# A two-layer hybrid encoder on one core: the first gate and up products are opened by token halves with spare buffers, and GpSimd makes the squares of the program's input and their sum

## The chip, the cores and the metric

The kernel runs on one NeuronCore of a Trainium2 chip. The metric is the time of one execution on the device in microseconds (us); a smaller one is better. The kernel before takes 2196.76 us, the median of three runs (2196.46 to 2197.05). Engines are called as in the profile: PE (matmuls), PEld (its weight loads), DVE (VectorE), ACT (ScalarE), POOL (GpSimd) and SP (SyncE, which here only issues DMAs).

## The reference

The input is 512 tokens of 1024 channels; 16 learned meta tokens are added, so that 528 token columns are worked on. Two layers each run a gated feed-forward block, a mixer (gated linear attention beside softmax attention, merged by gates) and a second feed-forward block. The change touches the start of the first feed-forward block alone:

```python
def rmsnorm(x, g):
    y = xf * lax.rsqrt(jnp.mean(xf * xf, axis=-1, keepdims=True) + EPS)
    return (y * g.astype(jnp.float32)).astype(x.dtype)

def swiglu(x, w_gate, w_up, w_down):
    return (jax.nn.silu(x @ w_gate) * (x @ w_up)) @ w_down

for l in range(DEPTH):
    h = h + 0.5 * swiglu(rmsnorm(h, norm_gains[l, 0]), ...)
    ...
```

## The kernel before

Channels lie on the 128 partitions, tokens in the free dimension: `h(c)` is chunk c of eight, 128 x 528 in float32. All of `h` stays in SBUF. Every matmul is made of three in a faster 32-bit format: an operand is split into a rounded part `hi` and the rest `lo`, and hi·hi, hi·lo and lo·hi are summed. ACT makes `hi` by a cast, DVE makes `lo` by a subtraction.

The gate and up products of a feed-forward block are made by a scheme of seven block products in place of eight. A pair of channel chunks and the two halves of 264 tokens form the 2 x 2 blocks b11, b12, b21, b22 of the input (first index: chunk of the pair, second: token half); four weight blocks "11", "12", "21", "22" of 512 KB each belong to a pair of output tiles. The products are named "1" to "7". Products "1", "2" and "4" take a weight block as it is loaded (11, 12, 22); "5", "6", "7" and "3" take sums of blocks: s1 = 21 + 22, s2 = 22 + s3, s3 = 21 - 11, s4 = s2 - 12. For the first pairs of output tiles these sums are made by DMAs that add into SBUF, issued by POOL (`Weights.add`, L209); ACT makes the negative that a sum starts from (`negative`, L204). In the text s3(0) is the sum s3 of pair 0 of output tiles, P0 6 is product "6" of that pair. One product is 24 matmuls of 128 x 264: four pairs of channel chunks, gate and up, three terms.

`ffn_steps` lists the products in the order in which PE runs them; the first block starts with P0 1, P0 2, P1 1, P1 2, P0 4, P1 4, P0 6, P0 5, P0 7. `Weights.fetch` issues the weight loads on SP ahead of use (L199), `make` splits a block into hi and lo (L290 on ACT, L291 on DVE). The input operands are made by `Norm.pair` (L512 to L531): it scales two whole chunks and makes all seven operands of that pair of chunks at once, seven hi/lo pairs in one tile `xc`.

The norm's factor 1/sqrt(mean of squares) is applied only after the products, so the squares are wanted late: `Norm.square` (L502 on ACT, the sum at L506 on DVE) is called for all eight chunks just ahead of P0 5, and after that product `norm.rs` has PE sum the accumulated squares over the partitions (`means`, two float32 matmuls, L474 in the profile) and makes the factor on ACT and DVE. That part is built with a high priority, so a scheduler, which orders each engine's instructions before the run, may place it ahead of things written before it. Each engine then runs its own list strictly in order and waits on semaphores.

Of the kernel before, what the change touches and what calls it, by code (L numbers as in the profile page):

```python
# [171 lines left out]
class Weights:  # L172
# [3 lines left out]
    def __init__(self, tc, raw, hi, lo, wts, win):  # L176
        nc = tc.nc
        self.tc, self.nc, self.raw, self.hi_pool, self.lo_pool, self.wts, self.win = tc, nc, raw, hi, lo, wts, win
        self.long = self.short = None
        self.loads = []  # L180
        for t, col in zip(PLAN, COLUMN):
            if t[0] == "op":
                self.loads.append(t[1:])
            elif col % SLAB == 0:
                self.loads.append(col // SLAB)
        self.at = {load: i for i, load in enumerate(self.loads)}
        self.made, self.fetched, self.got, self.summed, self.raws = 0, 0, {}, {}, {}
        self.pos = 0
        self.behind = None

    def dram(self, f, i, name):
        return self.win[((f[0] * 2 + f[1]) * NOP + i) * 4 + ("11", "12", "21", "22").index(name)]

    def block(self, f, i, name, pool=None, tag="raw"):

        w = (pool or self.raw).tile([P, SLAB], F32, tag=tag, name=f"w{name}_{f[0]}{f[1]}_{i}")
        first = f + (i, name) == (0, 0, 0, "11")
        for a in np.split(np.arange(SLAB), 2 if first else 1):
            self.nc.sync.dma_start(w[:, a[0] : a[-1] + 1], self.dram(f, i, name)[:, a[0] : a[-1] + 1])  # L199
        return w  # L200
# [5 lines left out]

    def add(self, t, src):

        self.nc.gpsimd.dma_start(t, src, accum_op=ALU.add)  # L209

    def chained(self, f, i):
        return i < 2 or f == (0, 0) and i < 4
# [1 line left out]
    def begin_sums(self, f, i, w=None):  # L214

        got = self.summed
        s3 = None
        if self.chained(f, i):
            s3 = self.negative(f, i, "s3", w)
            self.add(s3, self.dram(f, i, "21"))  # L220
        elif i < NPAIR:
            s3 = self.block(f, i, "21", self.long, "wsa")
        s2 = self.block(f, i, "22", self.short, "wsb")
        if self.chained(f, i):
            self.add(s2, s3)
        got[f, i, "7"], got[f, i, "6"] = s3, s2
        if (f, i) not in OPENING:
            self.first_sum(f, i)

    def first_sum(self, f, i):  # L230
        s1 = self.block(f, i, "21", self.short, "wsb")
# [44 lines left out]
    def make(self, upto):  # L276
        nc = self.nc
        while self.made < min(upto, len(self.loads)):
            self.fetch(self.made + 1)
            s = self.made  # L280
            load = self.loads[s]
            w = self.raws.pop(s, None)
            if w is None:
                w = self.summed.pop(load)
            hi = self.hi_pool.tile([P, SLAB], F32R, tag="whi", name=f"whi{s}")
            lo = self.lo_pool.tile([P, SLAB], F32R, tag="wlo", name=f"wlo{s}")
            for a in np.split(np.arange(SLAB), 2 if s == 0 else 1):
                cs = slice(a[0], a[-1] + 1)
                with self.tc.issue_after(self.behind) if self.behind else nullcontext():
                    nc.scalar.copy(hi[:, cs], w[:, cs])  # L290
                nc.vector.tensor_tensor(lo[:, cs], w[:, cs], hi[:, cs].bitcast(F32), ALU.subtract)  # L291
            self.got[s] = (hi, lo)
            self.got.pop(s - 12, None)
            self.made += 1
            if not isinstance(load, int) and load[2] in "126":
# [36 lines left out]
def build(tc, ctx, xt, wts, win, par, w2, const, umask, out):  # L332
# [155 lines left out]
    class Norm:  # L488


        def __init__(self, gc):
            self.gc, self.x, self.acc = gc, [], None

        def operand(self, c):
            hi, lo = slot("x", F32R), slot("x", F32R)
# [12 lines left out]
        def pair(self, j):  # L508
# [23 lines left out]
            parts(slice(4, 6), v2(t34))  # L532
            self.x.append((hi, lo))

        def chunk(self, c):
            self.operand(c)
            self.square(c)
# [35 lines left out]

    pending = [load_constants]

    def ffn(l, f, norm, done, following):

        x, rs, up, n = norm.x, None, None, live[0]
        w = n // 2
# [177 lines left out]
        for i, step in enumerate(steps):  # L757
            if step[0] == "P":
                if step[1:] == (0, "5") and norm.acc is None:
                    for c in range(KC):  # L760
                        norm.square(c)
                product_of_pair(*step[1:])
                if step[1:] == (0, "5"):
                    rs, up = norm.rs(True)
                    W.behind = prev_act[0]
                if step[1] in (2, 3) and step[2] in "6574":
                    m = next(risen)
                    V.scalar_tensor_tensor(h(m), h(m), -1.0, up, ALU.mult, ALU.mult)
                if i == last_op:
                    close_pools(norm.pools)  # L770
                    following()
            elif step[0] == "S":
                fast_down(*step[1:])
            elif step[0] == "O":
                g, last = step[1:]
                ks = slice(3, 4) if last else slice(0, 3)
                operands_of(g, ks, "152")
                difference(g, 0, 3, 0, ks)
                if last:
                    operand(g, "6")  # L780
            else:
                down(*step[1:])
        close_pools(pools)

    def project(x, rs, tag, f=1.0, n=T):
# [445 lines left out]
    def ending(sums, operand, rs):  # L1231
# [43 lines left out]
        factor(1)  # L1275
        leave(1, (0, 2, 4, 6))

    first = Norm(G_NORM)
# [8 lines left out]
    W.fetch(2)  # L1287
    first.pair(1)
    W.make(2)
    W.fetch(3)  # L1290
    first.pair(2)
    W.make(3)
    W.fetch(4)
    first.pair(3)
    nc.sync.dma_start(ct[:, C_O1024 : C_O1024 + P], const[:, C_O1024 : C_O1024 + P])

    norms = [first] + [Norm(G_NORM + i * KC) for i in range(1, 3 * DEPTH)]
    for l in range(DEPTH):
        a, b, c = norms[3 * l : 3 * l + 3]
        ffn(l, 0, a, b.chunk, lambda: operand_pools(b, "x"))  # L1300
# [79 lines left out]
```

## Time and profile before

| | |
|---|---|
| median of three runs | 2196.76 us |
| the profiled execution | 2196.04 us, span 2194.3 us |
| PE busy | 2157.0 us (98%) |
| PEld busy | 2066.7 us (94%) |
| DVE busy | 1777.9 us (81%) |
| ACT busy | 1215.5 us (55%) |
| POOL busy | 105.3 us (5%) |

The span is the stretch from the first to the last record of the profiled execution; the execution's own time is 1.74 us longer. In the views a row names the line of the kernel, the engine, the operation and the program's names of output and input (`xc<-t`), the number of such instructions (x2), and in brackets how long the engine sat idle before it and what ended that. A line of the kernel after the change is another than that of the same code before: L601 becomes L676 (products), L474 becomes L496 (means), L209 becomes L212 (adding DMAs), L290 and L291 become L304 and L305, L204 becomes L207.

### The profile page before, as it was taken

How to read it: one execution, taken by the hardware profiler on the slowest of the kernel's cores; microseconds unless marked ns; L12 is line 12 of the kernel's file. 1: busy time of each engine (PE TensorE's matmuls, PEld its weight loads, DVE VectorE, ACT ScalarE, POOL GpSimd, SP SyncE). 2: the span in 40 equal slices, each digit the busy share in tenths (PEclk: the TensorE clock that was granted, in tenths of full speed). 3: DMA queues.
4: the chain of work that ended last, by engine and by line, in shares of the span. 5: the costliest groups of instructions: out<-in, count | busy, mean ns of one | idle time of the engine just before them, and what ended most of it. 6: DMA issues, size and time to landing. Idle time of an engine off the chain costs nothing.

```text
span 2194.3 us, 40087 instructions
## 1 busy us (share of the span) xinstructions
PE 2157.0 (98%) x16506; PEld 2066.7 (94%) x16506; DVE 1777.9 (81%) x2699; ACT 1215.5 (55%) x1781; POOL 105.3 (5%) x124
## 2 busy tenths in 40 slices
PE   7999999999999999999999999999999999999998
PEld 7999999989999999999999999999788888999997
DVE  7887977586976689788799879785878767997987
ACT  8545545354784556454575455453557836554543
POOL 1100000000000000010010000000000001000100
PEclk9999999999999999999999999999999999999999
DMA  9866743212113567676667667432121145776752
GB/s 282 218 194 184 200 125 111 78 49 68 49 39 120 129 176 182 202 182 184 165 164 186 198 181 203 127 109 80 49 78 49 49 134 151 197 202 181 195 161 68
DMA packets 87751, 312.46 MB, mean 142 GB/s; under 512 B 9744, under 2 KB 12176, under 8 KB 87568
## 3 DMA queue, kind: packets, MB, share of 16 engines
q1 hardware_dynamic: 68336, 244.48, 33.6%
q0 software_dynamic: 17280, 62.92, 16.1%
q10 hardware_dynamic: 1952, 2.50, 0.4%
q8 instruction: 130, 2.13, 0.4%
q14 instruction: 53, 0.43, 0.1%
HBM read 289.94 MB, written 2.10 MB: 133 GB/s over the span
## 4 chain that ended last, share of the span: by engine, by line
PE 76%; DVE 16%; ACT 4%; issue 2%; DMA 2%; SPq 0%; POOL 0%; DVEq 0%; ACTq 0%
PE ss L601 33%; PE mm L468 13%; PE ss L721 11%; PE ss L468 10%; DVE wlo L291 4%; PE sm L468 2%; DVE g L687 1%; PE sm L1083 1%; DVE c L683 1%; DVE g L683 1%; PE ss L1058 1%; DVE c L651 1%; DMA w<-win 1%; DVE g L661 1%; PE ss L474 1%
## 5 line engine op out<-in xcount | busy, mean ns | idle before, releaser
L601 PE MATMUL ss<-xc,whi 128*128 128x264 f32 (+1 forms) x4928 | 903.4, 285 | 11.6 <-ACT whi L290 7.4
L601 PEld LDWEIGHTS ss<-xc,whi 128*128 128x128 f32 x4928 | 764.8, 189 | 14.9 <-ACT whi L290 7.8
L601 PE MATMUL ss<-xc,wlo 128*128 128x264 f32 (+1 forms) x2464 | 700.7, 285 | 3.4 <-DVE wlo L291 3.3
L601 PEld LDWEIGHTS ss<-xc,wlo 128*128 128x128 f32 x2464 | 465.1, 189 | 5.2 <-DVE wlo L291 5.2
L291 DVE TENSOR_TENSOR wlo<-w,whi 128x1024 fp32r<-128x1024 f32 (+1 forms) x335 | 405.5, 1217 | 64.1 <-ACT whi L290 63.9
L290 ACT CAST whi<-w 128x1024 fp32r<-128x1024 f32 (+1 forms) x335 | 345.9, 1048 | 159.8 <-PE ss L601 80.3
L468 PE MATMUL mm<-x,whi 128*128 128x264 f32 (+1 forms) x1712 | 384.8, 315 | 0.0
L468 PEld LDWEIGHTS mm<-x,whi 128*128 128x128 f32 x1712 | 278.4, 188 | 16.6 <-issue 1.0
L468 PE MATMUL mm<-x,wlo 128*128 128x264 f32 (+1 forms) x856 | 266.1, 315 | 0.0
L721 PE MATMUL ss<-g,whi 128*128 128x264 f32 (+1 forms) x1280 | 237.0, 284 | 0.0
L290 ACT CAST whi<-raw 128x1024 fp32r<-128x1024 f32 x126 | 132.1, 1049 | 163.5 <-PE mm L468 102.7
L605 ACT COPY c<-ss 128x528 f32<-128x528 f32 (+1 forms) x132 | 78.5, 595 | 245.7 <-PE ss L601 245.3
L291 DVE TENSOR_TENSOR wlo<-raw,whi 128x1024 fp32r<-128x1024 f32 x126 | 153.9, 1222 | 59.3 <-ACT whi L290 58.4
L721 PEld LDWEIGHTS ss<-g,whi 128*128 128x128 f32 x1280 | 198.4, 188 | 0.1
L721 PE MATMUL ss<-g,wlo 128*128 128x264 f32 (+1 forms) x640 | 181.3, 283 | 0.0
L468 PEld LDWEIGHTS mm<-x,wlo 128*128 128x128 f32 x856 | 159.6, 188 | 8.5 <-issue 0.7
L468 PE MATMUL ss<-g,whi 128*128 128x264 f32 (+2 forms) x900 | 166.2, 299 | 0.0
L468 PEld LDWEIGHTS ss<-g,whi 128*128 128x128 f32 x900 | 131.7, 188 | 5.2
L209 POOL DMA_DIRECT2D w<-win x60 | 52.7, 879 | 1557.1 <-DVE t L1211 392.2
L721 PEld LDWEIGHTS ss<-g,wlo 128*128 128x128 f32 x640 | 120.5, 188 | 0.0
L447 ACT ACTIVATE c<-c 128x528 f32<-128x528 f32 (+1 forms) x88 | 56.5, 642 | 96.3 <-DVE c L651 96.1
L291 DVE TENSOR_TENSOR wlo<-s,whi 128x1024 fp32r<-128x1024 f32 x86 | 104.9, 1220 | 1.7 <-ACT whi L290 1.5
(268 smaller groups left out, 3374.0 us busy)
## 6 DMA issues: line engine op xcount, KB each, us to landing
w<-win SPq DMA_DIRECT2D x333, 512.0 KB, 4.5
raw<-wts SPq DMA_DIRECT2D x126, 512.0 KB, 3.3
w<-win POOLq DMA_DIRECT2D x60, 512.0 KB, 7.4
s<-win POOLq DMA_DIRECT2D x26, 512.0 KB, 7.6
w<-s POOLq DMA_DIRECT2D x26, 512.0 KB, 6.0
s<-w POOLq DMA_DIRECT2D x8, 512.0 KB, 8.0
h<-xt SPq DMA_DIRECT2D x3, 528.0 KB, 6.6
out<-h ACTq DMA_DIRECT2D x4, 256.0 KB, 2.4
```

What stands on the lines that cost most here:

```text
L209: self.nc.gpsimd.dma_start(t, src, accum_op=ALU.add)
L290: nc.scalar.copy(hi[:, cs], w[:, cs])
L291: nc.vector.tensor_tensor(lo[:, cs], w[:, cs], hi[:, cs].bitcast(F32), ALU.subtract)
L447: prev_act[0] = S.activation(*args, **kw).ins
L468: TE.matmul(acc.half[i][:width], lhs, rhs[:, acc.spans[i]], start=first, stop=last)
L474: TE.matmul(a, weights, x[:, hs], start=True, stop=True)
L601: TE.matmul(acc[:, j], a[:, j, k], b[:, at], start=bool(begin and k == 0 and i == 0), stop=k == len(x) - 1 and i == 2, skip_group_check=no ...
L605: W.behind = S.copy(part(st, q), acc).ins
L651: V.scalar_tensor_tensor(td, ts, -0.5, rs[:, cs], ALU.mult, ALU.mult)
L661: V.tensor_tensor(raw[p // 4][2 * m + q][:, p % 4], t[:, q * w : (q + 1) * w], us, ALU.mult)
L683: V.tensor_tensor(lo, src[:, ks], hi.bitcast(F32), ALU.subtract)
L721: TE.matmul(acc[:, j], a[:, j, k], xs[b][:, k], start=bool(begin and k == 0 and i == 0), stop=k == 3 and i == 2, skip_group_check=not begin)
```

## The change

Before PE's first product a float32 tile of zeros is multiplied five times (`warm_up`). The input is loaded by token halves, the first halves of all chunks ahead of the second ones. Where `pair` made seven operands of a pair of chunks at once, `head` makes the two of the first token half (for products "1" and "2"), and later calls make the others: `fourth` (product "4"), `middle` ("5" and "6") and `rest` ("7" and "3"). They are called between products by the table `between`. Three weight blocks go into free buffers of the pool "g" (`SPARE`), so their loads wait for no release. The sums of the first two pairs are written by `open_sums` after P0 2 and after P1 2. `squares` takes the place of eight ACT squares and seven DVE additions: POOL multiplies each chunk by itself and adds it to a sum, in a buffer of the pool "g", fifteen dependent instructions of 128 x 528; it is called after P0 1. The rest of the program has the same instructions in the same order on each engine.

```diff
+WIDE = dict(raw=SLAB, wsa=SLAB, wsb=SLAB, g=2 * T)
+SPARE = ((0, 0), 1, "2"), ((0, 0), 0, "4"), ((0, 0), 1, "4")
...
+    def open_sums(self, f, i):
+
+        got = self.summed
+        with self.tc.issue_after(self.added) if self.added else nullcontext():
+            self.add(got[f, i, "7"], self.dram(f, i, "21"))
+        s2 = got[f, i, "6"] = self.second.pop((f, i), None) or self.block(f, i, "22", self.short, "wsb")
+        self.added = self.add(s2, got[f, i, "7"]).ins
+        self.first_sum(f, i)
+        self.add(got[f, i, "3"], s2)
...
-        if (f, i) in OPENING and product in "12":
-            (self.begin_sums if product == "1" else self.first_sum)(f, i, *[w] * (product == "1"))
-        if i < 2:
+        if (f, i) in OPENING:
+            if product in "12":
+                name, into = ("s3", "7") if product == "1" else ("s4", "3")
+                got[f, i, into] = self.negative(f, i, name, w)
+        elif i < 2:
...
-                self.raws[self.fetched] = self.block(*load[:2], DIRECT[load[2]])
+                self.raws[self.fetched] = self.block(*load[:2], DIRECT[load[2]], *[self.spare, "g"] * (load in SPARE))
...
-    nc.sync.dma_start(h(0), xt[:, 0])
+    nc.sync.dma_start(hall[:, 0:2, :HF], xt[:, 0:2, :HF])
...
+    def warm_up(n):
+        z = slot("rs")
+        V.memset(z, 0.0)
+        into = pair()
+        for i in range(n):
+            TE.matmul(into[:, i % 2, :HF], z[:, :P], z[:, P : P + HF], start=True, stop=True)
...
+        def head(self, j):
+
+            hi, lo = self.tiles()
+            for i in range(2):
+                src, g = h(2 * j + i, slice(0, live[0] // 2)), col(self.gc + 2 * j + i)
+                scaled_in = S.activation(hi[:, i], src, AF.Identity, scale=g).ins
+                V.scalar_tensor_tensor(lo[:, i], src, g, hi[:, i].bitcast(F32), ALU.mult, ALU.subtract)
+            return scaled_in
...
+        def squares(self):
+
+            both = twin("g")
+            for c in range(KC):
+                G.tensor_tensor(both[:, c > 0], h(c), h(c), ALU.mult)
+                if c:
+                    G.tensor_tensor(both[:, 0], both[:, 0], both[:, 1], ALU.add)
+            self.acc = both[:, 0]
...
+            for call in between.get(i, ()):
+                call()
...
-    nc.sync.dma_start(h(1), xt[:, 1])
-    first.pair(0)
-    W.fetch(1)
-    for c in (2, 4, 6):
-        nc.sync.dma_start(hall[:, c : c + 2], xt[:, c : c + 2])
-    W.make(1)
...
+    W.spare = slots["g"]
+    W.fetch(1)
+    load_x(2, 2, halves[0])
+    load_x(4, 4, halves[0])
+    W.fetch(4)
+    load_x(0, 4, halves[1])
+    load_x(4, 4, halves[1])
+    W.second[(0, 0), 0] = W.block((0, 0), 0, "22", W.short, "wsb")
+    W.fetch(6)
+    W.behind = first.head(0)
+    W.make(1, False)
+    W.behind = None
+    for j in range(1, KC // 2):
+        first.head(j)
+    W.sums((0, 0), 0, "1", W.last)
...
+    begin = [lambda i=i: W.open_sums((0, 0), i) for i in range(2)]
+    between = {0: [first.squares] + each(first.fourth, range(2)), 1: each(first.fourth, range(2, 4)) + begin[:1], 3: begin[1:] + each(first.middle),
+               4: each(first.rest)}
```

The built program shows where this puts POOL's instructions. Before, its list at the opening holds nothing but adding DMAs. In the names, s3_00_0 is s3(0), w22_00_0 becomes s2(0), w21_00_0 becomes s1(0), s4_00_0 is s4(0), and the digit after 00 is the pair of output tiles:

```order
L209 DMA s3_00_0_134<-win 128x1024
L209 DMA w22_00_0_137<-s3_00_0_134 128x1024
L209 DMA w21_00_0_168<-win 128x1024
L209 DMA s4_00_0_171<-w22_00_0_137 128x1024
L209 DMA s3_00_1_202<-win 128x1024
L209 DMA w22_00_1_205<-s3_00_1_202 128x1024
L209 DMA w21_00_1_276<-win 128x1024
L209 DMA s4_00_1_279<-w22_00_1_205 128x1024
```

After the change, from the second row of that list on (g14_205 is the buffer of the squares; an ISA instruction that reloads POOL's library stands ahead of the first square):

```order
L594 ISA
L594 TENSOR_TENSOR g14_205<-h_82 128x528 x2
L212 DMA w22_00_0_120<-s3_00_0_156 128x1024
L596 TENSOR_TENSOR g14_205<-g14_205 128x528
L212 DMA s3_00_1_176<-win 128x1024
L594 TENSOR_TENSOR g14_205<-h_82 128x528
L212 DMA s4_00_0_170<-w22_00_0_120 128x1024
L596 TENSOR_TENSOR g14_205<-g14_205 128x528
L212 DMA w21_00_0_295<-win 128x1024
L594 TENSOR_TENSOR g14_205<-h_82 128x528
L212 DMA w22_00_1_362<-s3_00_1_176 128x1024
L596 TENSOR_TENSOR g14_205<-g14_205 128x528
```

Behind the last of these rows stand four more squares and four more additions, eight instructions, and only then the adding DMAs of s1(1), s4(1) and s3(2). So nine of the fifteen instructions stand behind the DMA that adds s3(1) into s2(1), which used to be the sixth of POOL's list with no arithmetic around it.

On PE the means stood behind seven whole products and three matmuls of the eighth, P0 5 (whi7 is the weight of P0 5, whi6 that of P0 6):

```order
L601 MATMUL ss25_239<-xc21_214,wlo6_371 128x264
L601 MATMUL ss43_494<-xc3_104,whi7_411 128x264
L601 MATMUL ss43_494<-xc4_105,whi7_411 128x264
L601 MATMUL ss43_494<-xc3_104,wlo7_412 128x264
L474 MATMUL ss45_524<-t35_471,const_84 128x264 x2
L601 MATMUL ss43_494<-xc3_104,whi7_411 128x264
```

Now they stand after 13 of the 24 matmuls of P0 6, and read POOL's buffer:

```order
L676 MATMUL ss11_165<-xc6_139,whi6_378 128x264
L676 MATMUL ss11_165<-xc5_138,wlo6_379 128x264
L676 MATMUL ss11_165<-xc7_144,whi6_378 128x264
L496 MATMUL ss40_533<-g14_205,const_84 128x264 x2
L676 MATMUL ss11_165<-xc8_145,whi6_378 128x264
L676 MATMUL ss11_165<-xc7_144,wlo6_379 128x264
```

So 157 matmuls of products stand ahead of the means where 171 stood.

More of the change, by code (lines that the diff above doesn't have):

```diff
@@ L188, in __init__ @@
         self.pos = 0
-        self.behind = None
+        self.behind = self.spare = self.added = None
+        self.second = {}
     def dram(self, f, i, name):
@@ L207, in add @@
     def add(self, t, src):
-        self.nc.gpsimd.dma_start(t, src, accum_op=ALU.add)
+        return self.nc.gpsimd.dma_start(t, src, accum_op=ALU.add)
     def chained(self, f, i):
@@ L274, in fetch, with make @@
             self.fetched += 1
-    def make(self, upto):
+    def make(self, upto, summing=True):
         nc = self.nc
@@ L294, in make @@
             self.made += 1
-            if not isinstance(load, int) and load[2] in "126":
+            self.last = w
+            if summing and not isinstance(load, int) and load[2] in "126":
                 self.sums(*load, w)
@@ L533, in pair, with parts, tiles, fourth @@
             self.x.append((hi, lo))
+        def parts(self, j, at, src):
+            hi, lo = self.x[j]
+            S.copy(hi[:, at], src)
+            V.tensor_tensor(lo[:, at], src, hi[:, at].bitcast(F32), ALU.subtract)
+        def tiles(self):
+            w = live[0] // 2
+            self.x.append([slots["xc"].tile([P, 7 * T // 2], F32R, tag="xc", name=nm("xc"))[:, : 7 * w]
+                           .rearrange("p (s c) -> p s c", s=7) for _ in range(2)])
+            return self.x[-1]
+        def head(self, j):
[5 more added lines that the diff above has]
+            return scaled_in
+        def fourth(self, j):
+            w = live[0] // 2
+            raw, t, fourth = twin("g"), v2(slot("t")), slot("t")[:, :w]
+            for i in range(2):
+                S.activation(raw[:, i], h(2 * j + i), AF.Identity, scale=col(self.gc + 2 * j + i))
+            b11, b12, b21, b22 = [raw[:, i, a : a + w] for i in range(2) for a in (0, w)]
+            V.tensor_tensor(t[:, 0], b12, b11, ALU.subtract)
+            V.tensor_tensor(t[:, 1], b22, t[:, 0], ALU.subtract)
+            V.tensor_tensor(fourth, b21, t[:, 1], ALU.subtract)
+            self.parts(j, 5, fourth)
+            self.left.append((t, b12, b22))
+        def squares(self):
[5 more added lines that the diff above has]
+            self.acc = both[:, 0]
+        def middle(self, j):
+            self.parts(j, slice(2, 4), self.left[j][0])
+        def rest(self, j):
+            (hi, lo), (_, b12, b22) = self.x[j], self.left[j]
+            third = slot("t")[:, : live[0] // 2]
+            V.tensor_tensor(third, b12, b22, ALU.subtract)
+            self.parts(j, 4, third)
+            S.activation(hi[:, 6], b22, AF.Copy, scale=-1.0)
+            V.scalar_tensor_tensor(lo[:, 6], b22, -1.0, hi[:, 6].bitcast(F32), ALU.mult, ALU.subtract)
         def chunk(self, c):
@@ L574, in build, with ffn @@
     pending = [load_constants]
-    def ffn(l, f, norm, done, following):
+    def ffn(l, f, norm, done, following, between={}):
         x, rs, up, n = norm.x, None, None, live[0]
@@ L1276, in ending @@
         leave(1, (0, 2, 4, 6))
+    warm_up(5)
     first = Norm(G_NORM)
@@ L1280, in build, with load_x, each @@
     bp = [block_pools()]
-    nc.sync.dma_start(h(1), xt[:, 1])
-    first.pair(0)
+    def load_x(c, n, cs):
+        nc.sync.dma_start(hall[:, c : c + n, cs], xt[:, c : c + n, cs])
+    W.spare = slots["g"]
     W.fetch(1)
-    for c in (2, 4, 6):
-        nc.sync.dma_start(hall[:, c : c + 2], xt[:, c : c + 2])
-    W.make(1)
[L1287 to L1292, printed above, removed]
-    W.fetch(4)
-    first.pair(3)
-    nc.sync.dma_start(ct[:, C_O1024 : C_O1024 + P], const[:, C_O1024 : C_O1024 + P])
+    load_x(2, 2, halves[0])
+    load_x(4, 4, halves[0])
+    W.fetch(4)
+    load_x(0, 4, halves[1])
[8 more added lines that the diff above has]
+    W.sums((0, 0), 0, "1", W.last)
+    nc.sync.dma_start(ct[:, C_O1024 : C_O1024 + P], const[:, C_O1024 : C_O1024 + P])
+    def each(stage, js=range(KC // 2)):
+        return [lambda j=j: stage(j) for j in js]
+    begin = [lambda i=i: W.open_sums((0, 0), i) for i in range(2)]
+    between = {0: [first.squares] + each(first.fourth, range(2)), 1: each(first.fourth, range(2, 4)) + begin[:1], 3: begin[1:] + each(first.middle),
+               4: each(first.rest)}
     norms = [first] + [Norm(G_NORM + i * KC) for i in range(1, 3 * DEPTH)]
```

9 lines of the change are left out of this document (4 added, 5 removed).

## Prediction

> **What bounds the kernel now.** I read the page's head first, then the busy time by stretches of the opening, then the timelines of PE, POOL and DVE there.
>
> ```profile
> span 2194.3 us, 40087 instructions
> PE 2157.0 (98%) x16506; PEld 2066.7 (94%) x16506; DVE 1777.9 (81%) x2699; ACT 1215.5 (55%) x1781; POOL 105.3 (5%) x124
> ```
>
> PE is busy for all but 37 us. The stretches say where those are, and how many matmuls each holds (the figure in brackets):
>
> ```profile
> 0.00:10.00 10.00, 1.98 (x6) 1.44 (x6) 5.08 (x12) 7.27 (x13) 1.04 (x5) 1.00 0.83 290
> 10.00:20.00 10.00, 7.95 (x32) 6.52 (x31) 8.68 (x21) 8.90 (x17) 1.17 (x3) 1.00 1.03 345
> 20.00:30.00 10.00, 8.50 (x63) 7.86 (x64) 8.12 (x14) 8.77 (x15) 2.56 (x3) 1.00 1.08 269
> 30.00:40.00 10.00, 9.00 (x74) 8.78 (x73) 9.55 (x12) 9.68 (x15) 1.23 (x2) 1.00 1.03 300
> 40.00:50.00 10.00, 9.56 (x74) 9.46 (x75) 7.52 (x10) 6.71 (x9) 2.29 (x3) 1.00 1.02 204
> 80.00:100.00 20.00, 20.00 (x167) 20.00 (x166) 17.20 (x24) 14.00 (x17) 2.61 (x3) 1.00 0.75 175
> ```
>
> In full flow PE makes 167 matmuls in 20 us, 0.120 us each. Its first 40 us hold 175, which is 21 us of work: 19 us are lost, and an opening can win part of that. The rest of the program stays as it is, so the question is when PE has made a given number of matmuls after the opening. PE's own rows:
>
> ```profile
> 7.41 0.81 PE L601 MATMUL ss<-xc,whi 128*128 128x264 f32 x2 [7.41 <-ACT whi L290]
> 14.51 0.59 PE L601 MATMUL ss<-xc,whi 128*128 128x264 f32 x1 [0.22 <-DVE xc L520]
> 17.65 0.64 PE L601 MATMUL ss<-xc,whi 128*128 128x264 f32 x2
> 18.31 0.64 PE L601 MATMUL ss<-xc,whi 128*128 128x264 f32 x2
> 18.97 0.51 PE L601 MATMUL ss<-xc,whi 128*128 128x264 f32 x2
> 40.44 1.13 PE L474 MATMUL ss<-t,const 128*128 128x264 f32 x4 [1.45 <-ACT whi L290]
> ```
>
> PE starts at 7.41. Until about 18.97 three matmuls take 0.66 us (17.65 to 18.31), 0.22 each, so PE steps slowly in spite of the granted 1.00 in the stretches. The last row is the means: PE waits 1.45 us for it, and is done at 41.57 with 171 matmuls of products behind it. The row names ACT's cast, but DVE's sum of squares, which the means read, ends at 40.34:
>
> ```profile
> 33.89 1.51 DVE L506 TENSOR_TENSOR t<-t,t 128x528 f32<-128x528 f32 x2
> 36.46 3.88 DVE L506 TENSOR_TENSOR t<-t,t 128x528 f32<-128x528 f32 x5
> ```
>
> So the squares end just when PE wants them. That wait is where the change puts another engine.
>
> **The opening: a gain that has to pass the means.** Halving the first loads, making two operands in place of seven, the warm-up matmuls and the spare buffers all act ahead of the means. P0 6 stood in PE's list from 144 matmuls on, with the means 27 matmuls later. P0 6 needs s2(0), which below lands at 24.8; with a cast and a subtraction of 128 x 1024 (1.04 and 1.22) and 13 matmuls (1.6) PE could stand at the means by 28.7. If the squares were there, PE would end them at 29.8 with 14 matmuls fewer made (1.7): a gain of 41.6 - 31.5, about 10 us. All of these edits I cost at nothing, because PE then waits at the means; the cover is that wait, some 17 us below, and without it they would be the 10 us. Eight squares fewer on ACT and seven additions fewer on DVE (634 and 707 ns each, below: 5.1 and 4.9 us) win nothing either while PE waits for POOL. The rows by form:
>
> ```profile
> L506 DVE TENSOR_TENSOR t<-t,t 128x528 f32<-128x528 f32 x7 | 4.9, 707 | 0.5
> L502 ACT ACTIVATE t<-h 128x528 f32<-128x528 f32 x8 | 4.7, 634 | 0.0
> L204 ACT ACTIVATE s<-w 128x1024 f32<-128x1024 f32 x5 | 5.2, 1050 | 0.0
> L524 ACT ACTIVATE xc<-t 128x264 fp32r<-128x264 f32 x4 | 1.7, 418 | 0.0
> L290 ACT CAST whi<-w 128x512 fp32r<-128x512 f32 x2 | 1.1, 614 | 0.0
> L290 ACT CAST whi<-w 128x1024 fp32r<-128x1024 f32 x8 | 8.2, 1043 | 2.3 <-DMA w<-win 2.3
> L291 DVE TENSOR_TENSOR wlo<-w,whi 128x1024 fp32r<-128x1024 f32 x7 | 8.5, 1222 | 2.5 <-ACT whi L290 2.4
> L527 DVE TENSOR_TENSOR t<-t 128x264 f32<-128x264 f32 x4 | 1.7, 432 | 4.3 <-ACT t L512 4.3
> ```
>
> **POOL's list up to the ninth instruction from the end.** POOL works in order, and each of its DMAs waits for the landing of an earlier one:
>
> ```profile
> 4.01 1.36 ACT L512 ACTIVATE t<-h,par 128x528 f32<-128x528 f32 x2 [1.99 <-DMA par<-par]
> 9.17 1.01 POOL L209 DMA_DIRECT2D s<-win  x1 [8.72 <-ACT s L204]
> 19.01 0.87 POOL L209 DMA_DIRECT2D w<-s  x1 [8.83 <-DMA s<-win]
> 26.01 0.89 POOL L209 DMA_DIRECT2D s<-w  x1 [5.24 <-ACT whi L290]
> 26.55 1.25 POOL L209 DMA_DIRECT2D s<-win  x1
> 36.70 0.87 POOL L209 DMA_DIRECT2D w<-s  x1 [8.90 <-DMA s<-win]
> 45.02 0.97 POOL L209 DMA_DIRECT2D s<-win  x1
> 53.32 0.87 POOL L209 DMA_DIRECT2D w<-s  x1 [7.33 <-DMA s<-win]
> ```
>
> From s3's issue to the next row, which waits for it, are 9.84 and 10.15 us (19.01 - 9.17, 36.70 - 26.55). After the change ACT can begin at 4.01 as before (the parameters land then), and ahead of s3(0)'s negative stand four activations of 264, two casts of 512 and the negative: 4.01 + 4 x 0.42 + 2 x 0.61 + 1.05 = 8.0. So s3(0) is issued at 8.0 (before: 9.17) and has landed at 17.8. Until then POOL has time for the library instruction (no row shows its price; it is free up to some 5 us) and for the first two squares, since the second halves of the input are there by about 15: 2.2 MB of input, four blocks of 0.52 MB and a part of s3(0) make 4.5 MB, of which 2.9 MB move in the first 10 us (290 GB/s) and the rest at 345 GB/s. The block 22 for s2(0), moved behind them on SP, makes it 5.3 MB and gives 17, a cover of 0.8 us. At 17.8 POOL issues s2(0) (0.87), then one addition (1.25, below), then s3(1) at 19.9; this has landed at 30.1. Between them fit s2(0)'s landing (24.8, seven us after its issue as in the rows of before, where s4 followed s2 from 19.01 to 26.01), s4(0), s1(0) and three instructions of the squares: 24.8 + 2 x 0.88 + 2 x 1.25 = 29.1, a cover of 1.0. At 30.1 POOL issues s2(1), and at 30.9 the last nine instructions of the squares begin. No faster arithmetic can begin them earlier: the landing of s3(1) does that.
>
> **One instruction of the squares on POOL.** No row shows arithmetic of POOL on such tiles. Rows of the same operation on two engines:
>
> ```profile
> 0.24 0.10 POOL L1371 MEMSET const-float32-0.0<- 128x1 f32 x1 [0.24 <-issue]
> 0.81 0.06 DVE L404 MEMSET eps<- 128x1 f32 x1 [0.81 <-PEq L1371]
> L209 POOL DMA_DIRECT2D w<-win x6: 865/870/1224, 19.5 to 108.8; - x6
> L199 SPq DMA_DIRECT2D w<-win x18: 327/328/677, 1.7 to 52.1; - x18
> ```
>
> The lower end is DVE's own 0.71 us for the same addition. A memset takes POOL 1.67 times as long as DVE: 1.18 us. Issuing a DMA takes it 2.65 times as long as SP (870 against 328 ns): 1.87 us, the upper end. I take the memset's ratio, since it is the one of arithmetic engines, and 0.07 for each instruction's wait for the one before (DVE's five dependent additions take 3.88 us, 0.78 each, against 0.71): 1.25 us. Nine of them are 11.2 us (6.4 to 16.8).
>
> The Trainium skill (GPSIMD Engine Reference, Performance versus the Vector engine) gives an addition of 2048 elements as 4497 ns on GpSimd and 2293 ns on VectorE. By that ratio, 1.96, an instruction would take 1.39 us and the sum below would be 1.3 us higher, which is an estimate from that page; no row here shows it.
>
> **POOL and DVE in turns.** While POOL squares, DVE has work for the same memory: twelve instructions of 264 (`rest`, 0.43 each) and two subtractions of 1024 stand in its list in this stretch. No row shows both engines reading tiles at once. If they do not disturb each other this term is 0; if POOL waits out one short instruction of DVE before each of the nine, it is 9 x 0.43 = 3.9. Nothing in the trace excludes either, and I take 3.9, because DVE's queue is full there (9.55 of 10 us busy from 30 to 40 already before).
>
> The Trainium skill (SBUF — State Buffer, Who interferes with whom) states that a VectorE instruction with two inputs in SBUF and a GpSimd instruction that reads SBUF use one shared interface, and that the later one is blocked for the whole of the other. By that rule the term is there, and without it it would be 0; no run here shows it.
>
> **The sum.** The squares end at 30.9 + 11.2 + 3.9 = 46.0; the means (1.13) at 47.2, against 41.57: 5.6 later. The 14 matmuls that used to be done by then are still to do: 14 x 0.120 = 1.7. PE has stood idle from about 29 to 46. At the start of the program it stepped slowly after 7.41 us without work; from 14.51 to 18.97 it was nearly dense at 0.22 in place of 0.12, so that 45% of 4.46 us was lost. I add these 2.0 us once more (0 to 2.0: the idle 1.45 us at 40.44 brought no slow step back). Sum: 5.6 + 1.7 + 2.0 = 9.3 us slower.
>
> Behind the nine instructions stand the DMAs of s1(1), s4(1) and s3(2), and ACT's negative for s4(1) and s3(2) stands behind the norm's factor, so s3(2) goes out at about 55.7 where it was 45.02. With 8.3 us (53.32 - 45.02) and 10.2 us until ACT takes s2(2),
>
> ```profile
> 63.52 1.06 ACT L290 CAST whi<-w 128x1024 fp32r<-128x1024 f32 x1 [0.80 <-DMA w<-s]
> ```
>
> and 2.3 us to split it, P2 6 could begin at 76.5. PE comes there 203 matmuls (24.4 us) and the slow step (2.0) after 47.2: 73.6, or later with any other loss. I take 0 here and keep 0 to 2.9 for the range.
>
> The profiled execution before took 2196.04 us; with 9.3 that is 2205.3. The median of the runs lies 0.72 above it, so 2206.0.
>
> **Rivals.** First, not slower: POOL is as quick as DVE and undisturbed. Then the squares end at 30.9 + 6.4 = 37.3, the means at 38.4, and with 1.7 for the matmuls PE stands 1.5 us better than before, or 0.5 worse with the slow step: 2195.3 to 2197.3. It decides below about 0.87 us for each of the nine (0.65 with the slow step). For it speaks that most of POOL's time is waiting; against it the memset and the DMA rows. With an instruction of up to 1.1 us and no turns the time stays within 4.4 us of before. Chance 0.17. Second, slower still: the instruction takes 1.87 us and the turns come in full: 30.9 + 16.8 + 3.9 = 51.6, the means at 52.7, and 11.2 + 1.7 + 2.0 = 14.9, to which P2 6 may add 2.9: 2211.7 to 2214.6. For it speaks DVE's full queue, which also holds P0 6's own subtraction; against it, that DVE runs dry while PE stands. Chance 0.17. Third, the change does what it looks like, and the squares are off PE's path: then the 10 us of the opening come out, 2187. It needs nine instructions in no time behind the landing at 30.1. Chance 0.04.
>
> **How the numbers follow.** The forecast, 2206.0, has 0.62. Its own ends run from 2199 (0.9 us an instruction, no turns) to 2211 (1.5 us, turns, and the 2.9 at P2 6). The range reaches into the first rival to 2198.5 and through most of the second to 2214. A measurement of this kernel can tell about 0.2% (4.4 us) from no change: faster by more is the third rival, 0.04; within it the first, 0.17; slower the forecast and the second, 0.79.
>
> **What would show it.** Right: in the profile after, PE's longest wait of the opening stands before L496, 10 us or more, ended by POOL; PE's first product starts near 5.5 and P1 4 ends before 28; POOL's L594 and L596 follow each other at 1.1 to 1.8 us from 31 on; matmuls after the wait step at 0.22 for some microseconds. Wrong: if L496 starts before 40, or if L594 and L596 take 0.8 us or less, the term of the nine is too high; if DVE's instructions beside them keep their 0.43 and 1.22 us and POOL's gaps are nil, the turns are; if POOL reaches the last nine far from 30.9, the chain of landings is.

## The result, and the profile after

The kernel after takes 2208.32 us (median of six runs, 2207.54 to 2210.78) against 2197.27 us for six runs of the kernel before: 11.05 us slower, a ratio of 1.0052 (95% interval 1.0042 to 1.0063). Its profiled execution took 2208.42 us with a span of 2206.6, 12.38 us more than the profiled one before. Forecast were 2206.0, in a range of 2198.5 to 2214.0.

The stretches of the opening, with the same columns as before (PE with its matmuls, PEld, DVE, ACT, POOL, the granted clock, the DMA share, GB/s):

```profile
10.00:20.00 10.00, 9.25 (x72) 8.86 (x73) 7.43 (x13) 9.21 (x14) 2.93 (x4) 1.00 1.04 337
20.00:30.00 10.00, 3.73 (x21) 3.21 (x20) 9.79 (x15) 6.61 (x13) 4.76 (x6) 0.71 1.05 329
30.00:40.00 10.00, 7.34 (x44) 7.13 (x43) 10.00 (x6) 5.11 (x11) 9.77 (x9) 0.78 1.03 232
40.00:50.00 10.00, 4.74 (x16) 4.02 (x17) 10.00 (x12) 2.45 (x5) 8.42 (x7) 0.56 0.23 61
50.00:60.00 10.00, 10.00 (x78) 10.00 (x77) 8.94 (x12) 8.43 (x12) 1.75 (x2) 0.92 0.73 158
```

From 10 to 20 us PE now makes 72 matmuls where it made 32, so the opening does give a lead. Then it makes 21, 44 and 16 where it made 63, 74 and 74. Twice it stands, and DVE and POOL are both full. DVE's 10 us from 30 to 40 hold six instructions; before, its 9.55 held twelve. PE's own rows name four waits of note, and only the last is the one at the means (L496):

```profile
26.98 0.81 PE L676 MATMUL ss<-xc,whi 128*128 128x264 f32 x2 [5.42 <-ACT whi L304]
28.64 0.59 PE L676 MATMUL ss<-xc,wlo 128*128 128x264 f32 x1 [0.85 <-DVE wlo L305]
41.56 0.59 PE L676 MATMUL ss<-xc,wlo 128*128 128x264 f32 x1 [4.22 <-DVE wlo L305]
48.05 2.13 PE L496 MATMUL ss<-g,const 128*128 128x264 f32 x4 [3.70 <-POOL g L596]
```

The first is P0 4, the third P0 6, whose `lo` part DVE makes too late. The rows of DVE say why:

```profile
20.15 2.23 DVE L586 TENSOR_TENSOR t<-g,t 128x264 f32<-128x264 f32 x1
22.30 2.01 DVE L584 TENSOR_TENSOR t<-g 128x264 f32<-128x264 f32 x1
28.50 0.43 DVE L560 TENSOR_TENSOR xc<-t,xc 128x264 fp32r<-128x264 f32 x1
29.46 3.15 DVE L305 TENSOR_TENSOR wlo<-w,whi 128x1024 fp32r<-128x1024 f32 x1
32.54 6.96 DVE L560 TENSOR_TENSOR xc<-t,xc 128x528 fp32r<-128x528 f32 x4
39.43 2.08 DVE L305 TENSOR_TENSOR wlo<-w,whi 128x1024 fp32r<-128x1024 f32 x1
42.89 1.29 DVE L608 SCALAR_TENSOR_TENSOR xc<-g,xc 128x264 fp32r<-128x264 f32 x1
44.11 1.52 DVE L605 TENSOR_TENSOR t<-g 128x264 f32<-128x264 f32 x1
48.55 0.42 DVE L560 TENSOR_TENSOR xc<-t,xc 128x264 fp32r<-128x264 f32 x1
```

An instruction of 264 takes 0.43 us while POOL waits for a DMA, 1.29 to 2.23 while it squares, and 0.42 again when the squares are done. A subtraction of 1024 takes 3.15 and 2.08 in place of 1.22, and four subtractions of 528 take 6.96; the kernel with the squares on ACT, below, makes the same four in 2.56. Beside the squares, DVE makes one instruction for each one of POOL. POOL's rows at that time:

```profile
9.22 1.01 POOL L212 DMA_DIRECT2D s<-win  x1 [8.77 <-ACT s L207]
19.84 0.89 POOL L212 DMA_DIRECT2D w<-s  x1 [3.29 <-DMA w<-win]
20.45 1.62 POOL L596 TENSOR_TENSOR g<-g 128x528 f32<-128x528 f32 x1
22.33 1.68 POOL L594 TENSOR_TENSOR g<-h 128x528 f32<-128x528 f32 x1
29.26 0.91 POOL L212 DMA_DIRECT2D s<-w  x1 [5.24 <-DMA w<-s]
33.49 0.87 POOL L212 DMA_DIRECT2D w<-s  x1
34.10 1.62 POOL L596 TENSOR_TENSOR g<-g 128x528 f32<-128x528 f32 x1
45.41 1.14 POOL L594 TENSOR_TENSOR g<-h 128x528 f32<-128x528 f32 x1
46.63 1.37 POOL L596 TENSOR_TENSOR g<-g 128x528 f32<-128x528 f32 x1
47.94 0.87 POOL L212 DMA_DIRECT2D w<-win  x1
```

The last nine instructions run from 34.10 to about 48.0, 1.54 us each; the multiplication at 45.41 is followed by its addition after 1.22 us, and that by the DMA after 1.31.

The first wait, at P0 4, is lengthened in the same way. Its operands pass from DVE to ACT, and two of the DVE instructions ahead of them took 2.23 and 2.01 us beside POOL's rows at 20.45 and 22.33. In the kernel with the squares on ACT, below, the same instructions take 0.43 and PE waits 2.03 us there. So about 3.4 of the 5.42 us come from the squares.

The granted clock falls to half behind PE's pauses, from 24.2 to 34.3 and from 41.3 to 51.5. The same view for just these two stretches:

```profile
24.20:34.30 10.10, 6.46 (x27) 6.16 (x28) 9.89 (x15) 6.71 (x11) 5.04 (x6) 0.50 1.05 275
41.30:51.50 10.20, 6.24 (x22) 5.52 (x23) 10.09 (x13) 3.05 (x6) 7.20 (x6) 0.50 0.35 80
```

PE is busy for 6.46 and 6.24 us of them, and at half the clock that is half the work, 6.4 us of PE's time in all. Most of this does not lengthen the program. From 29.46 on DVE and POOL work without a pause and never wait for PE, so I take it that PE would have stood for DVE until 41.56 and for POOL until 48.05 at any clock. What counts is what follows 48.05: the means take 2.13 us in place of 1.13, and the matmuls behind them lose some 0.7. Before, no stretch of the opening shows less than 1.00. The Trainium skill (TensorE: Matmul & The Clock Gate, Part 1: The HAM clock gate) has the half clock follow at least one idle window of about 3.4 us, and full speed return after at least one busy window of that length. The two waits here, 5.42 and 4.22 us, are longer than that window, though the clock fell 2.7 us into the first, and shorter waits did the same in other runs (last section). The two stretches at half clock are three such windows long, 10.2 us each.

How many matmuls PE has made by a given time tells how the lead goes. The counts are sums of the stretches, without the ten records of the warm-up; the fifth column is of the last experiment that changes the opening:

| us | before | after | after less before | squares on ACT, s1(0) and `fourth` early |
|---|---|---|---|---|
| 20 | 38 | 86 | +48 | 86 (+48) |
| 30 | 101 | 107 | +6 | 122 (+21) |
| 40 | 175 | 151 | -24 | 194 (+19) |
| 50 | 249 | 167 | -82 | 253 (+4) |
| 70 | 412 | 326 | -86 | 395 (-17) |
| 160 | 1164 | 1079 | -85 | 1148 (-16) |

85 matmuls at 84 in 10 us are 10.1 us, and they stay lost. Of the other 2.3 us of the profiled executions' difference, up to 1.8 are one stretch of 20 us from 560 on with a granted clock of 0.91 (0.09 x 20), which the kernel before has at 1.00:

```profile
560.00:580.00 20.00, 20.00 (x155) 19.74 (x154) 16.27 (x41) 13.04 (x30) 0.00 (x0) 0.91 0.09 29
```

No step of the change reaches that far; the medians differ by 11.05.

### The profile page after: what moved, and what is told of

Its sections match the earlier page's. It is cut to its first block, busy times and chain, and to the rows that moved or that the text cites. A ratio compares the mean times of both kernels' runs of the same rounds, so it can differ in the third digit from the quotient of the medians.

```text
span 2206.6 us, 40121 instructions
## 1 busy us (share of the span) xinstructions
PE 2164.5 (98%) x16516; PEld 2073.4 (94%) x16516; DVE 1791.2 (81%) x2697; ACT 1212.5 (55%) x1777; POOL 125.3 (6%) x139
## 3 DMA queue, kind: packets, MB, share of 16 engines
q8 instruction: 130, 2.13, 0.4%
## 4 chain that ended last, share of the span: by engine, by line
PE 75%; DVE 16%; ACT 4%; issue 2%; DMA 0%; DVEq 0%; ACTq 0%
PE ss L676 33%; PE mm L490 13%; PE ss L796 10%; PE ss L490 9%; DVE wlo L305 4%; PE sm L490 2%; DVE g L762 1%; PE sm L1160 1%; DVE c L758 1%; DVE g L758 1%; PE ss L1135 1%; DVE c L726 1%; DVE g L736 1%; DVE h L804 1%; PE ss L496 1%
## 5 line engine op out<-in xcount | busy, mean ns | idle before, releaser
L676 PEld LDWEIGHTS ss<-xc,whi 128*128 128x128 f32 x4928 | 766.7, 189 | 11.3 <-ACT whi L304 5.6
```

Source lines behind the costliest of these rows:

```text
L676: TE.matmul(acc[:, j], a[:, j, k], b[:, at], start=bool(begin and k == 0 and i == 0), stop=k == len(x) - 1 and i == 2, skip_group_check=no ...
```

## Experiments

**The opening without POOL's squares.** ACT and DVE make the squares as before; all else is the change.

```diff
-    between = {0: [first.squares] + each(first.fourth, range(2)), ...
+    between = {0: each(first.fourth, range(2)), ...
```

> The change without POOL's squares: the opening by token halves, the spare buffers and the warm-up stay, the eight squares are made by ACT and their sum by DVE just ahead of P0 5, as before. If POOL's squares are what costs, all of the loss goes and the opening shows its own worth: 2187 to 2192 us, and no wait of PE over 3 us before the means. If the opening itself costs (P0 4 waits for operands that are made late, 5.4 us in the profile after), the time stays at 2200 or above.

Measured: 2204.76 us, against 2196.99 before, ratio 1.0036 (1.0022 to 1.0050). The opening alone loses 7.8 us where I had it gain. PE's waits and what stands behind them:

```profile
40.29 0.51 PE L676 MATMUL ss<-xc,whi 128*128 128x264 f32 x2 [3.58 <-ACT whi L304]
43.17 0.81 PE L676 MATMUL ss<-xc,whi 128*128 128x264 f32 x2 [2.37 <-ACT c L680]
39.19 1.04 ACT L304 CAST whi<-w 128x1024 fp32r<-128x1024 f32 x1 [6.21 <-DMA w<-win]
30.00 0.89 POOL L212 DMA_DIRECT2D s<-w  x1 [7.53 <-DMA w<-s]
30.54 1.25 POOL L212 DMA_DIRECT2D w<-win  x1
```

The weight of P0 5, s1(0), is a sum that POOL's DMA adds, and `open_sums` issues it behind s4(0), which waits 7.53 us for s2(0). So it goes out at 30.54 where the kernel before issues it at 19.55 (below); ACT gets it at 39.19, after 6.21 us without work, and the squares stand behind it in ACT's list. The same row of POOL in the kernel before:

```profile
19.55 1.22 POOL L209 DMA_DIRECT2D w<-win  x1
```

**POOL's squares in the old opening.** The kernel before, with the same fifteen instructions called after the first product:

```diff
                 product_of_pair(*step[1:])
+                if i == 0 and norm.acc is None and (l, f) == (0, 0):
+                    norm.squares()
```

> The kernel before with one edit: POOL makes the squares and their sum, called after P0 1; the opening is the old one. The scheduler puts the means 150 matmuls into PE's list. If POOL's squares cost by themselves: POOL ends them at about 40 to 44 (its list waits for s3(0) and s2(0) on the way), DVE's two-input instructions beside them are longer, and the time is 2199 to 2206 us. If they cost only together with the halved opening, the time stays within 2 us of before.

Measured: 2212.3 us, 15.3 above before, ratio 1.0072 (1.0059 to 1.0085): above both guesses. PE does not wait at the means at all; it waits 6.40 us for a `lo` part of DVE. One row of POOL and two of DVE below it show the other side:

```profile
40.40 0.59 PE L610 MATMUL ss<-xc,wlo 128*128 128x264 f32 x1 [6.40 <-DVE wlo L291]
19.80 7.33 POOL L539 TENSOR_TENSOR g<-h 128x528 f32<-128x528 f32 x1
21.58 1.23 DVE L291 TENSOR_TENSOR wlo<-w,whi 128x1024 fp32r<-128x1024 f32 x1
23.74 1.33 DVE L520 TENSOR_TENSOR xc<-t,xc 128x528 fp32r<-128x528 f32 x2
```

One multiplication of POOL took 7.33 us while DVE ran at its usual 1.23 and 0.70 without a gap. It ended when DVE paused; from then on the two took turns. So each holds up the other.

**Idle squares, idle memsets, idle copies, idle products.** Four kernels put work on POOL whose result nobody reads, while ACT and DVE make the real squares. In the first the change's own fifteen squares are made for nothing (`self.acc = both[:, 0]` becomes `self.idle = both`). In the others the kernel of the first experiment gets fifteen equal instructions behind s2(1):

```diff
+        if i == 1:
+            for _ in range(15):
+                with self.tc.issue_after(self.added):
+                    self.added = self.nc.gpsimd.memset(self.fill, 0.0).ins
```

or, in that last line, `tensor_copy(self.fill[:, 0], h(7))`, or `tensor_tensor(self.fill[:, 0], h(7), h(7), ALU.mult)`.

> POOL does all fifteen instructions of the squares as in the change, but nothing reads them; ACT and DVE make the squares that the norm uses. PE no longer waits for POOL at the means. If POOL and DVE block each other, P0 4 and P0 6 still get their operands late (DVE subtractions of 2 to 3 us, 128 x 528 instructions of about 1.7 us) and the time stays at 2199 to 2207. If the wait at the means is all, the time is that of the run with ACT's squares alone, 2187 to 2192.

> As the run with ACT's squares, and behind the DMA of s2(1) POOL makes fifteen idle memsets of 128 x 1056, which read nothing; the DMAs of s1(1), s4(1) and s3(2) stand among or behind them. If it is POOL's reading of tiles that blocks DVE, DVE's instructions beside the memsets keep 0.43, 0.70 and 1.22 us and the time is within 3 us of the run with ACT's squares alone. If POOL's occupation as such does it (late DMAs, any access to the memory), DVE's rows lengthen and the time is near that of the idle squares.

> The kernel with the idle POOL memsets (2204.4), its fifteen memsets replaced by fifteen idle copies of chunk 7 of h (128x528, one input read). If any reading of SBUF by POOL holds up DVE's two-input instructions: DVE rows beside the copies are lengthened as beside the squares (0.43 becomes 1.2 to 1.6, 1.22 becomes 2 to 3), and the time is 2206 to 2212. If only POOL's two-input instructions do: DVE's rows keep 0.43, 0.70 and 1.22, and the time is 2203 to 2206.

> As the kernel with idle copies, with fifteen idle multiplications of chunk 7 of h by itself (128x528) at the same place. If POOL's two-input reading is what holds up DVE: DVE's rows beside them are lengthened to two or three times, and the time is 2206 to 2213. If POOL's DMA list alone (s1(1), s4(1), s3(2) issued later) made the difference between squares and memsets: DVE's rows keep their length, and the time is 2203 to 2206.

| idle work on POOL | us | ratio to before | over the first experiment |
|---|---|---|---|
| none (first experiment) | 2204.76 | 1.0036 (1.0022 to 1.0050) | |
| memsets, 128x1056 | 2204.44 | 1.0035 (1.0023 to 1.0048) | -0.3 |
| copies, 128x528 | 2206.09 | 1.0042 (1.0028 to 1.0055) | +1.3 |
| products, 128x528 | 2213.86 | 1.0077 (1.0064 to 1.0090) | +9.1 |
| the change's squares | 2213.47 | 1.0076 (1.0064 to 1.0089) | +8.7 |

The idle squares came out above both guesses, the idle products just above theirs. Copies and products ran beside a kernel before of 2196.51 us, the others beside one of 2196.99; each against its own, copies are 1.8 and products 9.6 above the first experiment.

Memsets, copies and products begin at the same place of POOL's list, behind s2(1), with the same instructions in the same order on DVE and ACT. The later DMAs stand differently among them: that of s1(1) behind nine memsets, all fifteen copies or four products. DVE and POOL beside the memsets:

```profile
44.41 1.22 DVE L309 TENSOR_TENSOR wlo<-s,whi 128x1024 fp32r<-128x1024 f32 x1
45.54 4.78 DVE L532 TENSOR_TENSOR t<-t,t 128x528 f32<-128x528 f32 x6
44.33 3.39 POOL L242 MEMSET g<- 128x1056 f32 x3
```

Beside the copies:

```profile
41.14 0.85 DVE L609 TENSOR_TENSOR t<-g 128x264 f32<-128x264 f32 x1
44.23 1.64 DVE L309 TENSOR_TENSOR wlo<-w,whi 128x1024 fp32r<-128x1024 f32 x1
33.77 11.02 POOL L242 COPY g<-h 128x528 f32<-128x528 f32 x15
```

Beside the products, and PE's wait at the means there:

```profile
46.77 9.48 DVE L532 TENSOR_TENSOR t<-t,t 128x528 f32<-128x528 f32 x6
44.37 6.38 POOL L242 TENSOR_TENSOR g<-h 128x528 f32<-128x528 f32 x4
33.34 4.92 POOL L242 TENSOR_TENSOR g<-h 128x528 f32<-128x528 f32 x4
59.84 2.10 PE L500 MATMUL ss<-t,const 128*128 128x264 f32 x4 [8.44 <-issue]
```

Six additions of DVE take 4.78 us beside memsets and 9.48 beside products; a product of POOL takes 1.23 alone (4.92 for four) and 1.60 beside DVE. The last addition ends PE's wait of 8.44 us at the means. A copy of POOL also doubles DVE's 0.43 to 0.85, less than I had guessed (1.2 to 1.6), but is itself short (0.73), and the fifteen are over at 44.8, most of them while DVE stood, so that little of DVE's work met them here. So what holds DVE up is POOL reading SBUF; writing it costs nothing. POOL's later DMAs, the other candidate, are not it: beside the products s3(2) goes out at 62.10 in place of 53.54, but behind 62.2 PE's only named wait up to 120 us is one of 0.44, and the first experiment has one of 0.45 too. The Trainium skill's rule that the prediction weighed (SBUF — State Buffer, Who interferes with whom) holds here in all three: a POOL instruction that only writes is harmless, one that reads blocks a two-input instruction of DVE.

**s1(0) early.** The first experiment's kernel, with block 21 loaded ahead of the later blocks and its adding DMA placed right behind s2(0)'s:

```diff
+    W.first[(0, 0), 0] = W.block((0, 0), 0, "21", W.short, "wsb")
...
+        with self.tc.issue_after(self.added) if self.added and f == (0, 0) and i == 0 else nullcontext():
+            ins = self.add(s1, self.dram(f, i, "22")).ins
```

> As the run with ACT's squares, and the block 21 of s1(0) is loaded ahead of the two blocks 22 for product 4, with its adding DMA right behind that of s2(0) in POOL's list, ahead of s3(1) and s4(0). If what the halved opening loses is the landing of s1(0) (ACT stood 6.2 us at the cast for P0 5 until 39.2), PE waits no longer there, and the time falls below before: 2190 to 2195 us. If another late operand stands right behind it (s2(1) for P1 6, the squares that ACT begins late), little changes: 2199 to 2205.

Measured: 2200.04 us (11 runs), ratio 1.0014 (1.0005 to 1.0022). The time lies in the second guess's range, but it takes back 4.7 of the 7.8 us, and PE's wait of 3.58 us at P0 5 is gone. So the late s1(0), its load and its place in POOL's list, is the larger part of the opening's loss. PE's longest wait is now at P0 4:

```profile
26.30 1.75 PE L679 MATMUL ss<-xc,whi 128*128 128x264 f32 x4 [4.82 <-ACT whi L307]
18.59 0.60 ACT L683 COPY c<-ss 128x528 f32<-128x528 f32 x1 [2.96 <-PE ss L679]
```

Two more kernels start from this one. One also makes the squares on POOL as the change does; one leaves the warm-up out.

> The changed kernel, POOL's squares included, with the same early s1(0). The scheduler then puts the means behind P0 7, 215 matmuls into PE's list. If POOL's squares hold PE by themselves, through DVE's lengthened instructions (P0 4 and P0 6) and the last squares at about 48, the time stays at 2203 to 2211. If the late s1(0) was the loss of the change too, it falls to that of the run with ACT's squares and early s1(0), within 3 us.

> As the run with ACT's squares and early s1(0), without the five warm-up matmuls. If they win PE the faster step, the first three products step at 0.22 us for some 4 to 8 us and the time is 2 to 4 us above that run, unless a later wait hides it, in which case it is within 1 us.

With POOL's squares: 2215.88, ratio 1.0084 (1.0070 to 1.0098), 15.8 above the kernel without them and outside both guesses. PE waits 8.98 us at P0 4, 4.00 for a `lo` part, and 5.81 at the means:

```profile
61.11 2.13 PE L499 MATMUL ss<-g,const 128*128 128x264 f32 x4 [5.81 <-POOL g L599]
```

So in the change itself moving s1(0) wins nothing: this kernel is the slowest of all.

Without the warm-up: 2200.44, ratio 1.0016 (1.0007 to 1.0025). The wait at P0 4 is 4.82 us there too: the five products buy nothing here.

**P0 4's operands ahead of the copy.** In the row of ACT above, a copy of P1 1's result stands 2.96 us waiting for PE, with the eight activations for P0 4 behind it. In the first experiment the scheduler had that copy behind them, and the wait at P0 4 was 2.03 us. So 2.8 of the 4.82 us came with the early s1(0). Here the copy is put behind them again:

```diff
+                with tc.issue_after(first.raw_ins) if (l, f, p) == (0, 0, 1) else nullcontext(): snapshot(0)
```

> The kernel with squares on ACT/DVE and s1(0) added early (3.1 us slower than before), with one more edit: ACT copies P1 1's result out only behind its eight activations for P0 4's operands. Theory (what is left of the opening's loss is that P0 4's operands stand behind that copy on ACT, 4.8 us of PE's time): the wait before P0 4 falls below 2.5 us and the time is 2195 to 2198.5. Rival (the wait only moves, to the squares and the means, where PE already waited 2.1 us): the wait before P0 4 shrinks, the one at the means grows by as much, and the time stays 2199 to 2202.

Measured: 2200.2 us (11 runs), ratio 1.0016 (1.0007 to 1.0025): no gain, the rival's time by a part of the rival's way. The wait before P0 4 fell from 4.82 to 2.03 and 1.14, and the one at the means went from 2.09 to 1.79, so it did not move there. The lead of matmuls (the table above) falls from 48 to 21 between 20 and 30 us, to 4 between 40 and 50, where the wait at the means stands, and is gone by 70. A view of the clock and one of PE's rows behind the means:

```profile
24.40:31.20 6.80, 5.92 (x27) 5.92 (x28) 6.63 (x10) 5.41 (x10) 0.88 (x1) 0.50 1.04 272
51.19 0.39 PE L679 MATMUL ss<-xc,wlo 128*128 128x264 f32 x1 [1.01 <-DVE wlo L308]
```

The shorter wait is enough to halve the clock from 24.4 to 31.2, 3.0 us of PE's work. And from 50 to 70 PE makes 142 matmuls where it made 163 before. It waits 1.01, 0.46 and 0.97 us there, each time for a `lo` part of DVE, which is busy for 10.00 and 9.03 us of the two stretches; the DMA engines are full too (0.99 and 1.06), as they were before (0.96 and 1.05). Whether DVE's queue or the weights' loads keep a lead at 20 us from lasting was not tried and stays open.

No kernel of these is faster than the one before.

## Why the prediction was right, and where it was not

**The direction and the size** came out: 2208.32 where 2206.0 was forecast, and slower. The path did not. The forecast has PE stand once, some 17 us, at the means; it stood there for 3.70. That the time came so near is partly luck, as the sums below show. By experiments the 11.3 us over the 2196.99 of the first ones' before are 7.8 for the opening, 8.7 for POOL's squares beside DVE (idle squares less none), and 5.2 back (2213.47 - 2208.32). I put these 5.2 down to the squares that ACT and DVE then need not make, which no run shows by itself; the additions on DVE had been priced at 4.9.

**"An opening worth 10 us that has to pass the means"** failed. Without the squares the kernel loses 7.8 us, and the best of its openings still 3.1, so there was no gain for the means to cover, and the edits did not cost nothing. The step that failed is PE's standing at the means by 28.7: it took P0 6's weight and 13 matmuls, and not P0 4 and P1 4, whose operands need the second halves of the input, block 22 and a queue on ACT. P0 4 alone began at 26.98, and at 24.73 without POOL's squares. It also passed over s1(0), moved in POOL's list from 19.55 to 31.13 (30.54 without the squares), and the edit that moves it back is worth 4.7 as long as POOL makes no squares. The third rival, 2187, is out with it.

**POOL's list** was right in kind. s3(0) went out at 9.22 (8.0 forecast), s2(0) at 19.84 (17.8; the late block 22, whose cover was given as 0.8 us, held it for 3.29), s2(1) at 33.49 (30.1), and the nine began at 34.10 (30.9). What decided was not the landing of s3(1), for which POOL never waited, but the 5.24 us for s2(0) ahead of s4(0) and the squares behind it. The landing of s2(0) had been put at seven us after its issue, from a row whose wait ACT's cast had ended; it took 9.4 to the row that waits for it (19.84 to 29.26). The term of 0 for P2 6 held: s3(2) went out at 57.56 (55.7 forecast), and PE names no wait between the means and 130 us.

**One instruction** was sized well: 1.22 and 1.31 from start to start beside short DVE work, 1.25 forecast. The nine took 13.9 us where 11.2 and 3.9 made 15.1.

**The turns** are real, but were charged to the wrong engine. POOL lost little, since 1.22 beside 0.43 is its own 1.23. DVE lost 3.4 us from 20.15 to 24.4, which P0 4 waited for, and some 12 us from 29.46 to 48.2: 1.9 and 0.9 on two subtractions of 1024, 4.4 on four of 528, 1.1 on another of 264, and 3.9 on the four of 264 at 42.89 to 46.77. So the 17 us at the means became 5.42, 0.85, 4.22 and 3.70 at four places, and the sign named beforehand (10 us or more ahead of L496) was wrong. The spacing of L594 and L596 (1.2 to 1.7 us, once 2.2) and the slow matmuls came as named; P1 4's end ahead of 28 did not.

**The slow step** was forecast once with 2.0 us; it came twice. It took 6.4 us of PE's time, but only 1.7 behind the last wait: 1.0 in the longer means (2.13 us in place of 1.13) and 0.7 behind them.

In the prediction's own sum the means end at 50.18 against 41.57, 8.6 later (5.6 forecast), the 14 matmuls fewer are 1.7 as forecast, and the half clock from there to 51.5 takes 0.7 more (2.0 forecast). That is 11.0 against 9.3. The total was near, but partly by two errors that cancel: the opening, costed at nothing, loses 7.8, and the squares, costed at 9.3, add only 3.6 on top of that (2208.32 - 2204.76), since they wait and hold up where the opening waits anyway. In the old opening, and in the one with s1(0) early, the same squares cost 15.3 and 15.8.

## What to carry to other kernels

Before moving elementwise work to POOL, look at what DVE does at that time: beside POOL's reads each instruction of DVE with two inputs in SBUF waits for one of POOL's, so the price is DVE's queue and whoever waits for it, and not the moved work. When an opening is rewritten, follow every DMA of an in-order queue to its new place and ask who is next for its data; one adding DMA issued eleven microseconds later made more than half of this opening's loss. A lead of PE early on is worth nothing if what stands behind it comes no sooner: 48 matmuls ahead at 20 us were 17 behind at 70 in the last experiment above. And a pause of two microseconds in it can halve the clock behind it.

## What was not expected of the hardware

The half clock lasted whole multiples of about 3.41 us. In the first 100 us of all these kernels, summed over views of 0.1 us, the stretches are 3.41 (27.4 to 30.9, squares on ACT), 6.83 (24.3 to 31.2, the last experiment), 10.24 (twice in the change) and 17.07 (24.7 to 41.9, POOL's squares with s1(0) early), and no other length. So a pause that halves the clock costs in steps. How long the pause must be does not show: beside the idle products the clock fell 1.9 us into a wait of 2.03, with the squares on ACT it fell at 10.3, during a wait of 0.36 that followed one of 1.32, and a wait of 1.45 us before the change left it at 1.00.

DVE can shut POOL out as well: one product of POOL took 7.33 us beside a dense row of DVE instructions, of which two subtractions of 1024 kept their 1.23 us. And an instruction of DVE whose second input is a tile of matmul results keeps its length beside POOL (0.69 here, and 0.70 once each in two other runs). In the kernel with POOL's squares in the old opening, the first row is such an addition, the second DVE's neighbour with both inputs in SBUF, the third POOL's instruction at that time:

```profile
38.02 0.69 DVE L620 TENSOR_TENSOR c<-c,ss 128x528 f32<-128x528 f32 x1
36.80 1.29 DVE L531 TENSOR_TENSOR t<-t,t 128x264 f32<-128x264 f32 x1
37.88 1.38 POOL L541 TENSOR_TENSOR g<-g 128x528 f32<-128x528 f32 x1
```
